# The first microseconds of an encoder layer: first weight pieces on GpSimd's queue, one conversion on VectorE, another source for the warm-up, the identity made later

## The chip, the core and the metric

The kernel runs on one core of one Trainium2 chip. A core has TensorE (PE: matrix products, with PEld for loading the stationary operand), VectorE (DVE), ScalarE (ACT) and GpSimd (POOL), which work in parallel, each through its own instructions in order, and SyncE (SP), which here only issues transfers. Transfers between device memory and on-chip memory run on 16 transfer engines. Those issued by SP go through one queue (q1 in the profile), those issued by GpSimd through another (q0). The metric is the device time of one execution in microseconds; the time given for a kernel is the median over its runs.

## What is computed

One encoder layer on 1024 positions of 1024 channels, in float32: a SwiGLU feed-forward with 2752 hidden channels, a mixer (dilated window attention in three head groups beside a Fourier branch), a second feed-forward, each followed by a scaled residual sum and a layer norm.

```python
h = LN1(alpha*x + 0.5*SwiGLU_a(x))
h = LN2(alpha*h + HybridMixer(h))
h = LN3(alpha*h + 0.5*SwiGLU_b(h))
# SwiGLU(x) = (silu(x @ w_gate) * (x @ w_up)) @ w_down
```

Only the first products of SwiGLU_a, which use x and the first columns of its gate weights, are touched by most of the change.

## The kernel before

**Products.** Every float32 operand is split into a high part (rounded to the matrix engine's float32 form, tile names ending in h) and a low part (the rest, ending in l). A product is then three terms: high by high, high by low, low by high (`TERMS`). High parts are made by a copy, nearly always on ScalarE; low parts by a subtraction on VectorE, which needs the high part. Larger products are computed from seven block products instead of eight; the first block of x is called a11.

**Order.** Nothing in the program is ordered by hand beyond a few constants. The products are jobs in a fixed order for TensorE; the work on VectorE (`V`), ScalarE (`S`) and GpSimd (`G`), and the loads (`Q`), are nodes with dependences, an estimated duration, and a due time taken from the job that needs them. The class `Flow` walks through the jobs with an estimated clock for each engine and for the transfers and emits each node where it fits; each engine's instructions then run on the chip in the order in which they were emitted, and semaphores are derived from the tiles that they read and write. `pool_dma` issues a transfer on GpSimd and tells `Flow` that GpSimd is taken for 0.57 us. Half-size tiles come from a rotating pool of 14 (`half`), large ones from a pool of 46 pages.

**The first step.** The first feed-forward starts with three column blocks of the gate weights (`FIRST = 3`), 128 columns each, and the four 128-channel slices of a11: `first_step(k)` for k = 0 to 3 issues nine matmuls (three terms by three column blocks) into three banks called Aa. Its operands are four pieces of x (`xa`, 256 KB each, high parts Xa110h and Xa111h, two slices in each) and four weight pieces (`fw0` to `fw3`, 192 KB each, from `firsts_w`), made by `first_weights(k)`: a load on SP, a high part on ScalarE, a low part on VectorE. For k = 0 the 384 columns are cut at 128, so that the first column block is converted by an instruction of its own; the other pieces are converted whole. The loads of x and of the weights alternate on SP: x piece, weight piece, x piece, and so on. Behind them SP issues the other blocks of x (`in_xt`) and further weights (`lda`).

**The warm-up.** Before the first step TensorE multiplies a constant by itself eight times (line 2753, each a float32 matmul of 128 by 128 that the profile shows as two). The constant is `one`, a tile of one column that VectorE sets at line 334. The program's own preamble (line 2840) also sets constants on GpSimd, among them a float32 column of 1.0.

**The identity.** At lines 335 to 338 GpSimd counts (iota, tile `jp`, a half-size tile) and VectorE compares, which gives `ident`, a 128 by 128 identity that TensorE uses for transposes and GpSimd once at the very end. Its first reader is the transpose of the biases, `b_ps` (line 1299), whose operands GpSimd loads after the first product of the seventh pair of column blocks (`J[("a", 6), 1]`, numbered from 0) has been planned.

Of the kernel before, what the change touches and what calls it, by code (L numbers as in the profile page):

```python
# [12 lines left out]
AF = mybir.ActivationFunctionType  # L13
OP = mybir.AluOpType
AX = mybir.AxisListType

P = 128
# [27 lines left out]
FIRST = 3  # L45
# [36 lines left out]
class Flow:  # L82
# [22 lines left out]
    def V(self, *a, **kw):  # L105
        return self.task("V", *a, **kw)

    def S(self, *a, **kw):
        return self.task("S", *a, **kw)

    def G(self, *a, **kw):
        return self.task("G", 0.0, *a, **kw)
# [8 lines left out]
    def Q(self, need, mb, fn, deps=(), lead=24.0, **kw):  # L121
        self.loads.append(Node("Q", mb, fn, deps, need, lead, **kw))
        return self.loads[-1]

    def F(self, us, fn, deps=(), banks=0, **kw):
        self.floats.append(Node("F", us, fn, deps, banks=banks, **kw))
        return self.floats[-1]
# [162 lines left out]
class Builder:  # L290
# [7 lines left out]
    def page(self, name, dt=F32):  # L298
        return self.sb.tile([P, 1024], dt, name=name, tag="pg", bufs=NPG)

    def half(self, name, dt=F32):
        return self.sb.tile([P, 512], dt, name=name, tag="s2", bufs=NS2)
# [4 lines left out]
    def bank(self, name):  # L307
        return self.pp.tile([P, 512], F32, name=name, tag="ps", bufs=8)
# [6 lines left out]
def kernel(  # L315
# [6 lines left out]
    nc = tc.nc  # L322
    kb = Builder(ctx, tc)
    fl = Flow()
    page, half, bank = kb.page, kb.half, kb.bank
    V, S, G, Q, F, job = fl.V, fl.S, fl.G, fl.Q, fl.F, fl.job
# [3 lines left out]
    def as_k(t, kd=KD):  # L330
        return t.rearrange("p (k n) -> p k n", k=kd)

    one = kb.small([P, 1], "one")
    nc.vector.memset(one, 1.0)
    ident = kb.small([P, P], "ident")
    jp = half("jp", mybir.dt.int32)[:, :P]
    nc.gpsimd.iota(jp, pattern=[[1, P]], base=0, channel_multiplier=-1)
    nc.vector.tensor_scalar(ident, jp, 0.0, None, op0=OP.is_equal)
    zero = kb.small([P, 1], "zero")
    nc.vector.memset(zero, 0.0)  # L340
    ln_cols = kb.small([P, 32], "ln_cols")
# [3 lines left out]
    def pool_dma(*a, us=0.57, **kw):  # L345
        fl.queued(0.95 if "accum_op" in kw else us, 4e-6 * math.prod(a[0].shape))
        nc.gpsimd.dma_start(*a, **kw)  # L347
# [8 lines left out]
    W, B, H, J = {}, {}, {}, {}  # L356
# [245 lines left out]
    def first_weights(k, need, lead):  # L602

        st = {}

        def load():
            st["r"] = half(f"fw{k}")
            nc.sync.dma_start(st["r"][:, :FIRST * P], firsts_w[k])

        def hi(c0, c1):  # L610
            if c0 == 0:
                st["h"] = half(f"fw{k}h", F32R)
            nc.scalar.activation(st["h"][:, c0:c1], st["r"][:, c0:c1], AF.Copy)

        def lo(c0, c1):
            if c0 == 0:
                st["l"] = half(f"fw{k}l", F32R)
                FWP[k] = st["h"], st["l"]
            nc.vector.tensor_sub(st["l"][:, c0:c1], st["r"][:, c0:c1], st["h"][:, c0:c1].bitcast(F32))
        n, cuts = [(Q(need[0], 0.19, load, lead=lead, halves=1), -2.3)], [0, P, FIRST * P] if k == 0 else [0, FIRST * P]  # L620
        m = []
        for c0, c1 in zip(cuts, cuts[1:]):
            us = 0.15 + (c1 - c0) * 0.95e-3
            n = [S(us, lambda c0=c0, c1=c1: hi(c0, c1), n, need[k], tail=0.9, halves=int(c0 == 0))]
            m = [V(us, lambda c0=c0, c1=c1: lo(c0, c1), n + m, need[k], tail=0.2, halves=int(c0 == 0), hgives=int(c1 == cuts[-1]))]

    def lead_jobs(cs, X, nxt, steps=None):
# [650 lines left out]
    def mixer_consts():  # L1278
        st = {}

        def loads():
            st["raw"] = half("b_raw")[:56, :P]
            pool_dma(st["raw"], b_in.rearrange("(j p) -> j p", p=P))
            st["rb"], st["oh"] = kb.small([NUM_BUCKETS, NH], "rb"), half("oh")[:NUM_BUCKETS, :OH]
            pool_dma(st["rb"], rel_bias)
            pool_dma(st["oh"], c_onehot)
            pool_dma(chan, c_chan)
            pool_dma(ln_cols, c_ln)

        def rounded():  # L1290
            h, l = st["rbs"] = [kb.small([NUM_BUCKETS, NH], f"rb{x}", F32R) for x in "hl"]
            nc.vector.tensor_copy(h, st["rb"])
            nc.vector.tensor_sub(l, st["rb"], h.bitcast(F32))
            st["ohr"] = half("ohr", F32R)[:NUM_BUCKETS, :OH]
            nc.vector.tensor_copy(st["ohr"], st["oh"])

        def products():
            st["ps"], st["ln"] = bank("b_ps"), bank("ln_ps")
            nc.tensor.transpose(st["ps"][:, :56], st["raw"], ident[:56, :56])
            for i, w in enumerate(st["rbs"]):  # L1300
                nc.tensor.matmul(st["ln"][:NH, :OH], w, st["ohr"], start=i == 0, stop=i == 1)

        def columns():
            nc.vector.tensor_copy(b_cols, st["ps"][:, :56])

        def lines(g):
            line = half(f"line{g}")[:NH]
            nc.vector.memset(line, NEG_INF)
            nc.vector.tensor_copy(line[:, MID - HALFW:MID + HALFW + 1], st["ln"][:NH, g * NOFF:(g + 1) * NOFF])
            pool_dma(lines_d[:, g, :], line)  # L1310

        def shears(h):
            src = lines_d[h, h // SLOTS, :]
            pool_dma(shear_d[h], bass.AP(tensor=src.tensor, offset=src.offset, ap=[[0, P], [1, LINE]]))
        q = G(loads, [J[("a", 6), 1]], slack=20.0, halves=2)
        f = F(0.5, products, [V(0.7, rounded, [(q, 20.0)], halves=1)], 2, hgives=3)
        V(0.2, columns, [f], frees=1)
        for g in range(3):
            n = V(0.6, lambda g=g: lines(g), [f], frees=g // 2, halves=1)
            fl.later(n, 5.0, hgives=1)  # L1320
        return [G(lambda h=h: shears(h), [(n, 6.0 + 3.0 * h)]) for h in range(NH)]

    def reversed_rows():
        idx = kb.small([P, 2], "rev_idx", mybir.dt.int32)
        st, n = {}, G(lambda: pool_dma(idx, c_rev), [J[("a", 8), 1]], slack=20.0)
        for t in range(2):
            def gather(t=t):
                st[t] = page(f"rev{t}")
                fl.queued(1.06)
                nc.gpsimd.indirect_dma_start(out=st[t], out_offset=None, in_=w_pf,  # L1330
                                             in_offset=bass.IndirectOffsetOnAxis(ap=idx[:, t:t + 1], axis=0))

            def store(t=t):
                pool_dma(w_rev[t * P:(t + 1) * P, :], st[t])
            n = G(gather, [(n, 20.0)], slack=20.0, pages=1)
            n = G(store, [(n, 30.0)], slack=20.0)
            fl.later(n, 6.0, gives=1)
        return n

    shear_n = mixer_consts()  # L1340
    rev_n = reversed_rows()

# [51 lines left out]
    for i, (to, x0, x1) in enumerate((("t1", "b11", "b12"), ("t3", "b12", "b22"), ("t2", "t1", "b22"),  # L1394
# [6 lines left out]
        n = Q(J[("a", 1 + i), 4], 1.15, copy, [vtn[x0]] if x0 in vtn else [], lead=0.0)  # L1401
# [9 lines left out]
    for i, (to, x0, x1) in enumerate((("t1", "b11", "b12"), ("t3", "b12", "b22"), ("t2", "t1", "b22"),  # L1411
# [11 lines left out]
        n = Q(J[("a", 5 + i), 4], 0.6, copy, [ttn[x0]] if x0 in ttn else [], lead=0.0)  # L1423
# [31 lines left out]
    for p, bk, new in VORDER:  # L1455
        n = PROD[p][1]
# [255 lines left out]
    for i in range(2):  # L1712
        us = {}
# [383 lines left out]
    for i, (to, x0, x1) in enumerate((("t1", "b11", "b12"), ("t3", "b12", "b22"), ("t2", "t1", "b22"),  # L2097
# [6 lines left out]
        n = Q(SUMS0AT[i][0], 1.15, copy, [wtn[x0]] if x0 in wtn else [], lead=0.0)  # L2104
# [69 lines left out]
    for r, n in enumerate(("b11", "b21", "b22", "t1", "t3", "t2", "t4")):  # L2174
        for i in range(2):
            k = 4 * r + 2 * i
# [92 lines left out]
    for gi in range(4):  # L2269
        st = {}  # L2270
# [6 lines left out]
        for i in range(2):  # L2277
# [9 lines left out]
            def hi(gi=gi, i=i, st=st, views=views, t_=t_):  # L2287
                if (t_, i) not in fold:
                    t = page(f"fold{t_}{i}", F32R)
                    fold[t_, i] = t[:, 0:512], t[:, 512:1024]  # L2290
                pv = st["ps", i].rearrange("p (q m) -> p q m", q=4)
                nc.scalar.activation(next(views(i)), pv[:, :, 0:64], AF.Copy)
# [10 lines left out]
            n = S(0.42, hi, [f], pages=1 if s_ == 0 else 0, slack=2.0)  # L2303
# [43 lines left out]
    for t in range(2):  # L2347
        st = {}
# [68 lines left out]
    n = V(0.3, mid_edges, [f], frees=1, slack=2.0)  # L2417
    n = S(1.35, mid_hi, [n], slack=2.0)
# [18 lines left out]
    n = V(0.6, mid_raw, [PJ[2]], pages=1, slack=20.0)  # L2437
    n = S(1.06, mid_hi_w, [(n, 5.0)], pages=1)
# [83 lines left out]
    for c in range(8):  # L2522
        c2, cc = divmod(c, 2)
        st = {}
# [52 lines left out]
        n = S(0.62, sine, [FJ[c]], frees=int(c < 6 and c not in SINE.values()), halves=1)  # L2577
        (seeds if c > 5 else sines)[c - 6 if c > 5 else c] = [None, n]
        n = V(1.8, outs, [n], frees=2, hgives=1, pages=1)
# [4 lines left out]
    for c in range(8):  # L2584
        n, merge = four_out[c]
        n = V(1.38, merge, [n] + pj_n[c], gives=2, pages=2 if c % 2 == 0 else 0)
# [71 lines left out]
    for m in range(8):  # L2658
        n, y = norm_tile(lambda m=m: ya[m], lambda m=m: lw[m], done[m], f"y2_{m}", 2, 16.0 if m > 3 else -8.0)
# [89 lines left out]

    fl.seal()  # L2750
    junk = bank("warm")
    for i in range(8):
        nc.tensor.matmul(junk[:, :P], one.to_broadcast([P, P]), one.to_broadcast([P, P]), start=True, stop=True)
    fl.run()


# [97 lines left out]
```

## Time and profile before

| | us |
|---|---|
| median of 3 runs | 2012.93 |
| lowest, highest | 2012.84, 2013.2 |
| the profiled execution | 2013.17 |
| its span, first to last instruction | 2011.4 |
| busy in it: TensorE | 2005.1 |
| VectorE | 1402.3 |
| ScalarE | 883.7 |
| GpSimd | 366.0 |

The profiled execution's time is 1.77 us longer than its span; the profile's times count from the span's start. A row of the timeline gives the start, the duration, the engine, the line, the operation, the tiles (written from read), how many instructions are merged in it, and in brackets the idle time before it and what ended it. A row of waits names who waited, for whom, the total in us, how often, and the longest. A row of transfer issues gives the tiles, the queue, the count, the size of each, and the median time from issue to landing. In a row of the windows the stretch is followed by its sum, the busy time and the instructions of each engine, the granted TensorE clock, the busy share of the transfer engines and the GB/s that they moved.

### The profile page before, as it was taken

Reading aid. Unit: us, or ns where it says so; the run is one execution under the profiler, and the core shown is the slowest. Engines: PE = TensorE matmul, PEld = TensorE weight load, DVE = VectorE, ACT = ScalarE, POOL = GpSimd, SP = SyncE. Lnnn points to the kernel's source line nnn. Section 1 sums busy time; section 2 is a strip of 40 time slices with the busy share of each in tenths; the row PEclk is TensorE's granted clock in tenths of the full one; section 3 lists DMA queues with packets and bytes.
Section 4 is the critical chain, followed back from the end, with each engine's and each line's share of the span. In section 5 each row is a group of like instructions: output and inputs, shape, how many; then the busy total and the mean of one; then the engine's idle time right before and its main releaser. Section 6 shows DMA issues by size and latency. Waiting matters only on the chain.

```text
span 2011.4 us, 26489 instructions
## 1 busy us (share of the span) xinstructions
PE 2005.1 (100%) x9397; PEld 1680.9 (84%) x9397; DVE 1402.3 (70%) x2066; ACT 883.7 (44%) x1371; POOL 366.0 (18%) x616
## 2 busy tenths in 40 slices
PE   9999999999999999999999999999999999999998
PEld 8888888888888898888888888888888888888887
DVE  8765765577677878776776776877877665575566
ACT  6333333455445224565455445237533333354432
POOL 0133311111011032544443110000011111110000
PEclk9999999999999999999999999999999999999999
DMA  5789988799885286787667779873258877668753
GB/s 209 239 269 281 310 294 260 226 361 401 308 234 192 87 294 218 228 262 201 181 176 233 245 248 354 306 291 147 96 190 255 249 236 229 179 219 285 233 186 97
DMA packets 221829, 478.22 MB, mean 238 GB/s; under 512 B 44606, under 2 KB 95886, under 8 KB 221152
## 3 DMA queue, kind: packets, MB, share of 16 engines
q1 hardware_dynamic: 168736, 310.70, 45.0%
q0 software_dynamic: 52960, 165.82, 27.9%
q8 instruction: 74, 1.21, 0.2%
q14 instruction: 59, 0.48, 0.1%
HBM read 352.98 MB, written 193.68 MB: 272 GB/s over the span
## 4 chain that ended last, share of the span: by engine, by line
PE 100%; DVE 0%; DVEq 0%; issue 0%
PE Ab L541 14%; PE Aa L541 14%; PE Aq L541 8%; PE Db L541 6%; PE Da L541 6%; PE As L541 5%; PE Dq L541 3%; PE Zb L973 3%; PE Xb L973 3%; PE Za L973 3%; PE Xa L973 3%; PE Ds L541 2%; PE wA L2604 2%; PE pv L1939 2%; PE Vb L973 1%; PE Yb L973 1%
## 5 line engine op out<-in xcount | busy, mean ns | idle before, releaser
L347 POOL DMA_DIRECT2D pd<-px x128 | 78.9, 623 | 51.8 <-DVE px L1879 50.4
L347 POOL DMA_DIRECT2D n_spill<-y x16 | 9.4, 586 | 288.1 <-DVE y L1173 241.7
L347 POOL DMA_DIRECT2D hsba<-t2b x21 | 11.6, 551 | 266.5 <-DVE t2b L832 252.8
L347 POOL DMA_DIRECT2D hsaa<-t2a x21 | 12.9, 613 | 235.7 <-DVE t2a L832 230.0
L1870 ACT ACTIVATE p<-p,stat 128x192 f32<-128x192 f32 (+1 forms) x96 | 39.2, 410 | 28.1 <-DVE stat L1865 26.1
L828 DVE TENSOR_TENSOR t2b<-Db,t2b 128x512 f32<-128x512 f32 x21 | 14.5, 691 | 39.0 <-PE Db L541 39.0
L735 ACT ACTIVATE t2b<-Ab 128x512 f32<-128x512 f32 x21 | 12.6, 600 | 63.8 <-PE Ab L541 63.8
L735 ACT ACTIVATE t2a<-Aa 128x512 f32<-128x512 f32 x21 | 12.6, 600 | 61.6 <-PE Aa L541 61.6
L828 DVE TENSOR_TENSOR t2a<-Da,t2a 128x512 f32<-128x512 f32 x21 | 14.5, 689 | 34.0 <-PE Da L541 34.0
L2694 POOL TENSOR_SCALAR zd<-ident,ls 128x128 f32<-128x128 f32 x1 | 0.4, 375 | 202.1 <-DVE ls L2703 202.1
L1158 ACT ACTIVATE y<-ya,ls 128x1024 f32<-128x1024 f32 x16 | 18.4, 1149 | 36.6 <-DVE ls L1153 26.0
L820 DVE TENSOR_TENSOR t3b<-Db,t3b 128x512 f32<-128x512 f32 x21 | 14.5, 691 | 22.2 <-PE Db L541 20.7
L820 DVE TENSOR_TENSOR t3a<-Da,t3a 128x512 f32<-128x512 f32 x21 | 14.5, 691 | 21.7 <-PE Da L541 20.6
L541 PE MATMUL Da<-Xs40h,usa 128*128 128x512 f32 x84 | 29.3, 389 | 0.0
L541 PE MATMUL Da<-Xs41h,usa 128*128 128x512 f32 x84 | 29.3, 389 | 0.0
L541 PE MATMUL Db<-Zs40h,usb 128*128 128x512 f32 x84 | 29.3, 389 | 0.0
L541 PE MATMUL Db<-Zs41h,usb 128*128 128x512 f32 x84 | 29.3, 389 | 0.0
L347 POOL DMA_DIRECT2D gate_d<-os x16 | 8.6, 538 | 94.2 <-ACT os L1629 69.7
L347 POOL DMA_DIRECT2D y_spill<-n x16 | 8.8, 549 | 91.5 <-DVE n L1189 91.4
L735 ACT ACTIVATE t3b<-Ab 128x512 f32<-128x512 f32 x21 | 12.6, 600 | 26.0 <-PE Ab L541 25.8
L735 ACT ACTIVATE t3a<-Aa 128x512 f32<-128x512 f32 x21 | 12.6, 598 | 22.7 <-PE Aa L541 22.6
L1634 DVE SCALAR_TENSOR_TENSOR oq<-Dq,b_cols,t2q 128x512 f32<-128x512 f32 x12 | 11.8, 986 | 13.3 <-PE Dq L541 13.3
(7711 smaller groups left out, 7543.0 us busy)
## 6 DMA issues: line engine op xcount, KB each, us to landing
qa<-hsas SPq DMA_DIRECT2D x43, 256.0 KB, 5.7
qa<-tdat SPq DMA_DIRECT2D x43, 256.0 KB, 5.2
qb<-hsbs SPq DMA_DIRECT2D x43, 256.0 KB, 3.9
ga<-in_ffn_gu_dram SPq DMA_DIRECT2D x21, 512.0 KB, 8.8
ua<-in_ffn_gu_dram SPq DMA_DIRECT2D x21, 512.0 KB, 9.3
gb<-in_ffn_gu_dram SPq DMA_DIRECT2D x21, 512.0 KB, 4.8
ub<-in_ffn_gu_dram SPq DMA_DIRECT2D x21, 512.0 KB, 6.8
qb<-tdbt SPq DMA_DIRECT2D x33, 256.0 KB, 4.3
```

What stands on the lines that cost most here:

```text
L347: nc.gpsimd.dma_start(*a, **kw)
L541: nc.tensor.matmul(out, pick(w, a)[:, k * P:(k + 1) * P], self.cols(xn, b, k), start=first and k == 0 and ti == 0, stop=last and k == kt - ...
L735: nc.scalar.activation(H[c, t], B[c, "B"], AF.Copy)
L820: nc.vector.tensor_sub(H[c, "t3"], B[c, "D"], H[c, "t3"])
L828: nc.vector.tensor_sub(H[c, "t2"], B.pop((c, "D")), H[c, "t2"])
L973: nc.tensor.matmul(bank_, a, b, start=first and ti == 0, stop=last and ti == len(todo) - 1, skip_group_check=True)
L1158: nc.scalar.activation(st["y"], st["a"], AF.Square, bias=s[:, 2:3], scale=1.0, accum_out=s[:, 3:4])
L1634: stt(views(pages_[i], hf), views(b, None), bias[i], views(H.pop((c, t)), None), op0=OP.add, op1=op)
L1870: nc.scalar.activation(p3()[:, i, :], p3()[:, i, :], AF.Exp, bias=stats[h][:, k, 0:1], scale=1.0, accum_out=stats[h][:, k, 1:2])
L1939: nc.tensor.matmul(out, v, pt[:, sl * P:(sl + 1) * P], start=start, stop=stop, skip_group_check=True)
L2604: nc.tensor.matmul(B["w", bk, m], X4.cols(xn, a, k)[:, m * P:(m + 1) * P], pick(w, b), start=new and k == 0 and ti == 0, stop=k == 3 and t ...
L2694: nc.gpsimd.tensor_scalar(st["d"], ident, s()[:, 0:1], -1.0 / D, op0=OP.mult, op1=OP.mult)
```

## The change

Four things are changed.

- The four first weight pieces are issued by GpSimd (`pool_dma`) instead of SP. The four first x pieces and all later loads stay on SP.
- Where a high part of a first weight piece ends at column 128, which is the first cut of piece 0 alone, it is made by VectorE with a copy instead of by ScalarE; the planner gets it as a node of VectorE.
- The warm-up multiplies the preamble's float32 constant, broadcast to 128 by 128, instead of the tile `one`; the memset of `one` goes.
- The identity isn't made at the start. `identity()` registers a node for GpSimd (the iota, after the first product of pair ("a", 6), with its half-size tile taken from the planner's pool) and one for VectorE (the compare) behind it.

```diff
-    one = kb.small([P, 1], "one")
-    nc.vector.memset(one, 1.0)
     ident = kb.small([P, P], "ident")
-    jp = half("jp", mybir.dt.int32)[:, :P]
-    nc.gpsimd.iota(jp, pattern=[[1, P]], base=0, channel_multiplier=-1)
-    nc.vector.tensor_scalar(ident, jp, 0.0, None, op0=OP.is_equal)
...
             st["r"] = half(f"fw{k}")
-            nc.sync.dma_start(st["r"][:, :FIRST * P], firsts_w[k])
+            pool_dma(st["r"][:, :FIRST * P], firsts_w[k])
 
         def hi(c0, c1):
             if c0 == 0:
                 st["h"] = half(f"fw{k}h", F32R)
-            nc.scalar.activation(st["h"][:, c0:c1], st["r"][:, c0:c1], AF.Copy)
+            if c1 == P:
+                nc.vector.tensor_copy(st["h"][:, c0:c1], st["r"][:, c0:c1])
+            else:
+                nc.scalar.activation(st["h"][:, c0:c1], st["r"][:, c0:c1], AF.Copy)
...
-            n = [S(us, lambda c0=c0, c1=c1: hi(c0, c1), n, need[k], tail=0.9, halves=int(c0 == 0))]
+            n = [(V if c1 == P else S)(us, lambda c0=c0, c1=c1: hi(c0, c1), n, need[k], tail=0.9, halves=int(c0 == 0))]
...
+    def identity():
+        jp = {}
+
+        def count():
+            jp["t"] = half("jp", mybir.dt.int32)[:, :P]
+            nc.gpsimd.iota(jp["t"], pattern=[[1, P]], base=0, channel_multiplier=-1)
+        n = G(count, [J[("a", 6), 1]], slack=20.0, halves=1)
+        V(0.3, lambda: nc.vector.tensor_scalar(ident, jp["t"], 0.0, None, op0=OP.is_equal), [(n, 1.0)], slack=20.0, hgives=1)
+
+    identity()
     shear_n = mixer_consts()
...
     junk = bank("warm")
+    ones = nc.const_aps.tensor(1.0, (P, P))
     for i in range(8):
-        nc.tensor.matmul(junk[:, :P], one.to_broadcast([P, P]), one.to_broadcast([P, P]), start=True, stop=True)
+        nc.tensor.matmul(junk[:, :P], ones, ones, start=True, stop=True)
```

## The prediction

> **What bounds the kernel now.** I read the page first, then the table of waits for TensorE, then the timeline of the first 14 us.
>
> ```profile
> span 2011.4 us, 26489 instructions
> PE 2005.1 (100%) x9397; PEld 1680.9 (84%) x9397; DVE 1402.3 (70%) x2066; ACT 883.7 (44%) x1371; POOL 366.0 (18%) x616
> ...
> PE zr L2697 <- POOL zd L2694: 1.4, 1, 1.4
> PE warm L2753 <- DVE one L334: 0.9, 1, 0.9
> ...
> 0.28 0.10 POOL L2840 MEMSET const-float32-1.0<- 128x1 f32 x1
> ...
> 0.73 0.39 SPq L1244 DMA_DIRECT2D xa<-in_firsts_dram  x1
> 0.81 0.06 DVE L334 MEMSET one<- 128x1 f32 x1 [0.81 <-PEq L2840]
> 0.84 0.23 POOL L337 IOTA jp<- 128x128 int32 x1 [0.40 <-POOLq L2840]
> ...
> 0.92 3.79 PE L2753 MATMUL warm<-one 128*128 128x128 f32 x16 [0.92 <-DVE one L334]
> 1.11 0.23 DVE L338 TENSOR_SCALAR ident<-jp 128x128 f32<-128x128 int32 x1 [0.24 <-POOL jp L337]
> 1.18 0.42 SPq L608 DMA_DIRECT2D fw<-in_firsts_w_dram  x1
> ...
> 3.46 0.63 ACT L395 ACTIVATE Xa110h<-xa 128x512 fp32r<-128x512 f32 x1 [1.45 <-DMA xa<-in_firsts_dram]
> ...
> 4.00 0.60 ACT L613 ACTIVATE fw0h<-fw 128x128 fp32r<-128x128 f32 x2
> 4.01 0.43 SPq L608 DMA_DIRECT2D fw<-in_firsts_w_dram  x1
> 4.12 0.69 DVE L401 TENSOR_TENSOR Xa110l<-xa,Xa110h 128x512 fp32r<-128x512 f32 x1 [2.77 <-ACT Xa110h L395]
> ...
> 4.36 1.63 PE L599 MATMUL Aa<-Xa110h,fw0h 128*128 128x512 f32 x3
> 4.49 0.43 SPq L1244 DMA_DIRECT2D xa<-in_xt_dram  x1
> ...
> 5.79 1.46 PE L599 MATMUL Aa<-Xa110l,fw0h 128*128 128x512 f32 x3
> 6.10 0.63 ACT L395 ACTIVATE Xa110h<-xa 128x512 fp32r<-128x512 f32 x1 [1.50 <-DMA xa<-in_firsts_dram]
> 6.64 0.51 ACT L613 ACTIVATE fw1h<-fw 128x384 fp32r<-128x384 f32 x1
> ...
> 7.07 0.88 PE L599 MATMUL Aa<-Xa110h,fw0l 128*128 128x512 f32 x3
> 7.79 0.86 PE L599 MATMUL Aa<-Xa110h,fw1h 128*128 128x512 f32 x3
> ...
> 14.08 0.40 PE L541 MATMUL Aa<-Xa120h,lda0h 128*128 128x512 f32 x1
> ```
>
> TensorE works in 2005.1 of 2011.4 us, and its whole list of waits is two rows: 0.9 us before the warm-up and 1.4 us behind the last tile. All that the change can gain therefore lies in the first microseconds, and all that it could lose later would have to be a wait that the kernel does not have now.
>
> In those first microseconds three things follow one another. The first piece of x is awaited until 3.46 and its high part made by 4.09 (3.46 + 0.63). ScalarE then makes fw0h in two parts, until 4.60. TensorE starts its first useful product at 4.36, when the first part is there. From 7.79 to 14.08 lie 27 products (steps 1 to 3, nine each): 0.233 us each. From 5.79 to 7.07 lie three: 0.427 us each. So TensorE runs its first six products at not much over half its later pace, and the full pace begins at about 7.07, 6.15 us after the warm-up began. Step 0 (nine products) takes 7.79 - 4.36 = 3.43 us where the full pace would need 9 x 0.233 = 2.10. From 4.36 to 5.79 there are 1.43 us for three products, 1.28 at the slow pace: 0.15 us went to waiting for the second part of fw0h.
>
> One microsecond of earlier start in the slow stretch is 1/0.427 = 2.34 products more before the pace changes, each of which saves 0.233 us behind it: **an earlier start is worth 0.545 of itself**, and so is a late one.
>
> **The change part by part.** The profiled execution took 2013.17 us, its span and 1.77 us around it; the median of the three runs is 2012.93, 0.24 less. The sum is made as a difference against the profiled execution, and then put on the median.
>
> *Warm-up with the preamble's constant.* The constant 1.0 is written by 0.38, so the wait for VectorE's memset (0.81 to 0.87) is gone. What is left is the start of the program, which releases SP at 0.73. The warm-up starts about 0.17 earlier, at 0.75, and with its 3.79 us ends at about 4.54. The useful products don't wait for it then. If the full pace also comes 0.17 earlier, that is worth 0.17 x (1 - 0.233/0.427) = 0.08; if not, nothing. I take 0.04.
>
> *Four weight pieces on GpSimd's queue.* Removed from SP are four issues of 0.42 to 0.43 us. SP's later issues move up by one to four slots of about 0.47: the second x piece by one, the first large x transfer from 4.49 to about 2.6. GpSimd no longer has the iota at its start, so its first issue comes at about 0.80 and the four take these durations:
>
> ```profile
> 60.83 0.75 POOL L347 DMA_DIRECT2D hsaa<-t2a  x1 [59.75 <-DVE t2a L832]
> 71.48 0.56 POOL L347 DMA_DIRECT2D hsaa<-t2a  x1 [9.90 <-DVE t2a L832]
> ...
> xa<-in_firsts_dram SPq DMA_DIRECT2D x1, 256.0 KB, 2.7
> fw<-in_firsts_w_dram SPq DMA_DIRECT2D x1, 192.0 KB, 2.7
> ...
> out_dram<-z SPq DMA_DIRECT2D x1, 256.0 KB, 2.1
> ...
> hsbs<-sab POOLq DMA_DIRECT2D x2, 256.0 KB, 2.3
> ...
> DMA to landing us min/median/max: 2.5/4.6/7.6
> ...
> chan<-in_c_chan_dram POOLq DMA_DIRECT2D x1, 256.0 KB, 7.1
> ...
> 3.00:4.00 1.00, 1.00 (x6) 1.00 (x6) 0.00 (x0) 0.54 (x2) 0.00 (x0) 1.00 1.04 261
> 4.00:5.00 1.00, 1.00 (x6) 0.97 (x5) 0.88 (x3) 0.60 (x3) 0.00 (x0) 1.00 0.89 152
> 5.00:6.00 1.00, 1.00 (x4) 0.81 (x3) 0.35 (x2) 0.00 (x0) 0.00 (x0) 1.00 0.89 313
> ```
>
> The first GpSimd issue of the program takes 0.75, a later one 0.56: they end at 0.80 + 0.75 + 3 x 0.56 = 3.23. The fourth piece is issued at about 2.7 instead of 4.01. No load by GpSimd into an idle machine is in the trace. The nearest rows: a 256 KB store by GpSimd in a quiet stretch lands in 2.3 us, one by SP in 2.1; GpSimd's loads of a bias tile (the line of minimum, median and maximum) land in 2.5 at the least and 4.6 in the median; the load of chan, queued behind others, took 7.1. SP's own two first loads take 2.7. I take 2.7 to 3.1 for the first weight piece, near the quiet rows, because nothing but the first x piece is then in flight: it lands at 3.5 to 3.9, against 1.18 + 2.7 = 3.88 now. The ends are 3.3 (0.80 + 2.5) and 7.9 (0.80 + 7.1).
>
> What it costs: the first x piece (256 KB, landed at 3.43) has the transfer engines to itself today, and the weight piece follows. Now both are in flight together. At worst they share evenly and both land when the second of them lands now, at 3.88; the same bytes need the same time. Then Xa110h is made from 3.91 to 4.54 and TensorE starts at 4.57. At best the x piece is undisturbed and TensorE starts at 4.12. I take the middle, 4.35. The pieces for step 1 have room: fw1h is ready at 6.64 + 0.51 = 7.15 and is needed at 7.79. The three windows (their last two numbers) show the transfer engines busy at 0.89 to 1.04 while only 152 to 313 GB/s flow, so earlier issues on SP mostly wait in a queue that is full already.
>
> The Trainium skill ("DMA: Bandwidth & Descriptors", Specifications) speaks against this part: it puts the first byte of a GpSimd transfer at about 1 us and of an SP one at about 0.6. By that estimate the piece lands 0.4 later than on SP, at 3.9, and the start is 4.57; the rows show 0.2 between the two queues.
>
> *First high part on VectorE.* Removed from ScalarE: the first of the two fw0h instructions. Added to VectorE: a conversion of 128 columns.
>
> ```profile
> L1295 DVE CAST ohr<-oh 32x388 fp32r<-32x388 f32 x1 | 0.3, 344 | 0.0
> L1292 DVE CAST rbh<-rb 32x12 fp32r<-32x12 f32 x1 | 0.2, 154 | 0.0
> ```
>
> Between 0.154 for 12 columns and 0.344 for 388, that is 0.21. VectorE is idle until 4.12, so it runs beside Xa110h. ScalarE's second part, 0.40, then follows Xa110h directly and is ready 0.40 after it, before the second product asks for it (0.427): the 0.15 us of waiting are gone. Behind the new instruction on VectorE stands Xa110l, which the fourth product needs 1.28 us after the start; the copy and Xa110l together take 0.90 from the landing, so this never binds. Should Xa110l stand ahead of it in the order, fw0h would come at 5.0; the planner counts the weight piece as there before it counts Xa110h as made, so I don't expect that.
>
> *Identity in the sixth pair.* An iota of 0.23 on GpSimd and a compare of 0.23 on VectorE leave the start and come back near 111 us.
>
> ```profile
> DVE t12a6l L372 <- ACT t12a6h L367: 1.1, 1, 1.1
> ...
> L1299 PE MATMUL b_ps<-ident,b_raw x1: 265/265/265, 142.1 to 142.1; 56*128 56x56 f32 x1
> ```
>
> VectorE idles 1.1 us before one instruction there, GpSimd had idled 9.90 us before its issue at 71.48 and idles as long between its groups, and the identity is first read at 142.1, some 30 us later. Cost nothing; without that cover 0.23 us on VectorE. At the start it frees GpSimd before its first issue, counted above.
>
> *Sum*: start at 4.35 and no gap, (4.36 + 0.15 - 4.35) x 0.545 = 0.09 gained, with 0.04 from the warm-up 0.13. At the ends: start 4.12 with the earlier pace gains 0.21 + 0.08 = 0.29, start 4.57 without it loses 0.03. From 2013.17 that gives 2013.04; on the median, **2012.8**, with 2012.6 to 2013.0 as its own bounds and 0.3 more on each side for runs that spread from 2012.84 to 2013.2.
>
> **The rivals.**
>
> *R1, the weight piece lands late, nothing else.* For: 4.6 us is GpSimd's median in the bias row. It would land at 5.4 and TensorE start at about 5.67, (5.67 - 4.51) x 0.545 = 0.63 lost; a landing at 4.9 loses 0.36. Against: those loads ran beside others. Time 2013.2 to 2013.6.
>
> *R2, slower: a hole in TensorE's work holds the slow pace longer.* Place: between the end of the warm-up, now 4.54, and the first product. Today there is none, since 4.36 lies before the warm-up's end at 4.71. It decides from the point where the weight piece lands after about 4.3 (4.54 less the copy's 0.21), which the forecast's late end just touches. If the hole restarts the 6.15 us, a start at 5.2 brings the full pace at 11.35 instead of 7.07: 4.28 x 0.454 = 1.94, with 0.38 for the late start 2.3. Time **2015.2**. Against: the landing must be late and the count must restart, and no row shows either.
>
> *R3, the full pace a whole step earlier.* The warm-up starts 0.17 earlier; if the pace changes in steps of a clock that the kernel doesn't set, this may reach an earlier one, before step 0. Then its nine products take 2.10 instead of 3.43: 1.33 less, and 2011.5. For: the runs differ by 0.36 among themselves. Against: 0.17 is small beside 6.15.
> The Trainium skill ("TensorE: Matmul & The Clock Gate", The HAM clock gate) gives a free-running window of about 3.4 us that must be busy before full speed. With a start at 0.92 full speed would come between 4.3 and 7.7; the 7.07 here agrees. By it R2 costs one window, 3.4 x 0.454 = 1.5, so 2014.8, and R3 stays possible.
>
> *R4, the rest of the order changes.* The planner decides by estimated times, and a changed start may shift later decisions. For: VectorE, ScalarE and GpSimd get other estimates. Against: TensorE waits for nothing in the middle of the kernel, so there is slack for small shifts. A weight load issued so late that its landing lies bare costs up to 8.8 us:
>
> ```profile
> ga<-in_ffn_gu_dram SPq DMA_DIRECT2D x21, 512.0 KB, 8.8
> ```
>
> That would be 2021.7; the likelier size is below 2.
>
> **How the numbers follow.** Forecast 0.65, R1 0.11, R2 0.11, R3 0.08, R4 0.05. The predicted time is the forecast's, 2012.8. The range 2011.4 to 2013.9 holds the forecast, R1 and R3; R2 and R4, 0.16 together, are left out. A measurement of this kernel can tell 0.2%, 4.0 us, from no change. No case gains that much: the start holds 1.33 us of slow pace and 0.9 of waiting in all. Faster 0.02, for what I have not seen; slower 0.04, the heavy end of R4; the rest is within.
>
> **What would show it.** In the timeline after: the four fw issues on GpSimd between 0.8 and 3.2; the warm-up from about 0.75; fw0h on VectorE before Xa110l; the first useful product at 4.1 to 4.6 and step 1 at 7.5 to 7.8. The identity near 111 us with VectorE waiting as before. A first product after 5 shows R1, products of 0.427 us after 8 us show R2, products of 0.233 in step 0 show R3, and a new row among TensorE's waits shows R4. A time beyond 2013.9 with none of these, or a gain beyond 1.5 us, would prove the reading wrong.

## The result and the profile after

| | kernel before | changed kernel |
|---|---|---|
| median, us | 2012.93 (2012.22 to 2013.65, 14 runs) | 2016.99 (2014.89 to 2019.2, 14 runs) |
| ratio | 1 | 1.0021, 95% interval 1.0014 to 1.0028 |
| profiled execution: time, span | 2013.17, 2011.4 | 2017.23, 2015.5 |

The change costs 4.06 us, in the medians and in the two profiled executions alike. The changed kernel also spreads more: 4.3 us between its fastest and slowest run, against 1.4.

First the table of TensorE's waits in the changed kernel (engine, line, what it waited for: us in total, times, longest).

```profile
PE Aa L594 <- DVE fw0h L609: 2.5, 1, 2.5
PE zr L2705 <- POOL zd L2702: 1.4, 1, 1.4
PE warm L2762 <- PEq L2849: 0.8, 1, 0.8
PE sc L1842 <- DVE oq L1642: 0.2, 1, 0.2
```

A new wait leads it, 2.5 us in front of the first step, for the high part of the first weight piece. The timeline of the changed kernel shows how it came about (start, duration, engine, line, tiles, idle before and releaser; line 342 issues GpSimd's transfers, 609 is the conversion on VectorE, 594 the first steps).

```profile
0.73 1.81 SPq L1242 DMA_DIRECT2D xa<-in_firsts_dram  x4
...
0.77 3.74 PE L2762 MATMUL warm<-const-float32-1.0 128*128 128x128 f32 x16 [0.77 <-PEq L2849]
...
1.29 2.35 POOL L342 DMA_DIRECT2D fw<-in_firsts_w_dram  x4 [0.85 <-POOLq L2849]
...
3.38 0.63 ACT L390 ACTIVATE Xa110h<-xa 128x512 fp32r<-128x512 f32 x1 [1.37 <-DMA xa<-in_firsts_dram]
...
6.64 0.23 DVE L609 CAST fw0h<-fw 128x128 fp32r<-128x128 f32 x1 [5.74 <-DMA fw<-in_firsts_w_dram]
...
7.01 0.95 PE L594 MATMUL Aa<-Xa110h,fw0h 128*128 128x512 f32 x3 [2.50 <-DVE fw0h L609]
...
7.78 1.47 PE L594 MATMUL Aa<-Xa110l,fw0h 128*128 128x512 f32 x3
...
9.04 1.48 PE L594 MATMUL Aa<-Xa110h,fw0l 128*128 128x512 f32 x3
...
10.32 1.26 PE L594 MATMUL Aa<-Xa110h,fw1h 128*128 128x512 f32 x3
...
11.42 0.84 PE L594 MATMUL Aa<-Xa110l,fw1h 128*128 128x512 f32 x3
...
16.86 0.39 PE L536 MATMUL Aa<-Xa120h,lda0h 128*128 128x512 f32 x1
```

From the view of the tile fw, the time from issue to landing of the four weight pieces:

```profile
DMA to landing us min/median/max: 5.3/6.5/7.3
```

GpSimd's first issue comes at 1.29, not 0.80, and the first piece is there at 6.64, 5.3 after its issue. The x piece is not delayed: its high part starts at 3.38, against 3.46 before. The warm-up ends at 4.51, so TensorE has nothing to do for 2.50 us. Then a second thing happens: the first three products run at the full pace, and from 7.78 to 11.2 TensorE is back at half. The view by stretches of 1 us says the same in the granted clock (stretch, then busy shares with counts of PE, PEld, DVE, ACT and POOL, the granted TensorE clock, the transfer engines' share, GB/s).

```profile
4.00:5.00 1.00, 0.51 (x3) 0.23 (x2) 0.00 (x0) 0.01 (x1) 0.00 (x0) 1.00 0.65 189
5.00:6.00 1.00, 0.00 (x0) 0.00 (x0) 0.00 (x0) 0.00 (x0) 0.00 (x0) 1.00 0.97 309
6.00:7.00 1.00, 0.00 (x0) 0.02 (x1) 0.36 (x2) 0.36 (x2) 0.00 (x0) 1.00 0.97 374
7.00:8.00 1.00, 0.99 (x4) 0.89 (x5) 1.00 (x4) 0.57 (x2) 0.00 (x0) 0.89 1.03 371
8.00:9.00 1.00, 1.00 (x3) 0.76 (x3) 0.78 (x3) 0.73 (x2) 0.00 (x0) 0.50 0.98 381
...
11.00:12.00 1.00, 1.00 (x5) 0.79 (x5) 0.64 (x3) 1.00 (x2) 0.00 (x0) 0.90 1.05 397
```

(The column reads 1.00 also where the clock record has not begun yet; the pace of the products shows the half clock of the first microseconds.) The trace's clock records put the full clock at 4.37 to 7.78, half at 7.78 to 11.20 and full from there on: 3.413 us each. In the kernel before, the full clock begins at 7.08 and stays until after the last product.

At the first product on lda0h the changed kernel is 2.78 us late (16.86 against 14.08 in the prediction's rows). This stays constant to within 0.1 us until about 900 us; TensorE then loses 0.8 more, and the rest is lost at the end. The last rows, of the changed kernel and then of the kernel before, are:

```profile
2009.92 1.13 PE L2705 MATMUL zr<-ln3g,zd 128*128 128x512 f32 x2 [1.42 <-POOL zd L2702]
```
```profile
2006.33 1.12 PE L2697 MATMUL zr<-ln3g,zd 128*128 128x512 f32 x2 [1.42 <-POOL zd L2694]
```

That is 3.59 late. The span is 4.1 longer, so 0.5 is lost behind the last product. So the three losses are **2.8 at the start, 0.8 near 900 us, 0.5 behind the end**; the experiments ask what belongs to which part of the change.

### The profile page after: what moved, and what is told of

The parts are those of the page before. It is cut to its first block, busy times and chain, and to the rows that moved or that the text cites. A ratio compares the mean times of both kernels' runs of the same rounds, so it can differ in the third digit from the quotient of the medians.

```text
span 2015.5 us, 26493 instructions
## 1 busy us (share of the span) xinstructions
PE 2006.1 (100%) x9397; PEld 1681.0 (83%) x9397; DVE 1402.2 (70%) x2066; ACT 884.5 (44%) x1370; POOL 367.6 (18%) x620
## 4 chain that ended last, share of the span: by engine, by line
PE 98%; DVE 1%; DMA 1%; SPq 0%; issue 0%; ACT 0%; DVEq 0%; POOLq 0%
PE Ab L536 14%; PE Aa L536 14%; PE Aq L536 7%; PE Db L536 6%; PE Da L536 6%; PE As L536 5%; PE Za L971 3%; PE Zb L971 3%; PE Xb L971 3%; PE Xa L971 3%; PE Dq L536 3%; PE Ds L536 2%; PE wA L2612 2%; PE pv L1947 2%; PE Vb L971 1%; PE Yb L971 1%
```

## The experiments

The theory was that GpSimd's queue brings the first piece late, which starts the work late and opens a hole that lets the clock fall. Against it stood: that the other three parts of the change carry some of it; that the early x pieces now crowd the transfer engines, whatever the queue; that the piece is merely too large; and, from the second group of runs on, a rival about the loss near 900 us. The times, each beside the kernel before on the same chip:

| run | what differs from the changed kernel | median us (range) | ratio, 95% interval |
|---|---|---|---|
| e0_after | nothing | 2017.13 (2015.59 to 2018.28) | 1.0021, 1.0012 to 1.0030 |
| e1_sp | weight pieces on SP | 2013.21 (2012.73 to 2014.31) | 1.0003, 0.9994 to 1.0012 |
| e5_act | weight pieces on ScalarE's queue | 2012.64 (2012.29 to 2015.53) | 1.0001, 0.9992 to 1.0010 |
| e2_pool_only | the other three parts undone | 2016.9 (2014.31 to 2018.17) | 1.0018, 1.0009 to 1.0027 |
| e4_first_on_sp | first piece alone on SP | 2014.34 (2014.01 to 2015.5) | 1.0008, 0.9999 to 1.0017 |
| e6_split_first | first piece in two transfers | 2018.13 (2017.06 to 2019.15) | 1.0024, 1.0014 to 1.0034 |
| e3_warm20 | 20 warm-up products | 2018.08 (2017.21 to 2019.69) | 1.0026, 1.0016 to 1.0037 |
| e11_pool_wide8 | 8 warm-up products, 320 columns | 2015.57 (2014.87 to 2017.94) | 1.0015, 1.0006 to 1.0024 |
| e8_sp_warm20 | on SP, 20 warm-up products | 2017.89 (2016.52 to 2019.61) | 1.0025, 1.0015 to 1.0034 |
| e9_sp_wide8 | on SP, 8 of 320 columns | 2014.98 (2014.22 to 2015.52) | 1.0011, 1.0002 to 1.0020 |
| e10_sp_narrow20 | on SP, 20 of 48 columns | 2021.76 (2019.52 to 2022.71) | 1.0045, 1.0032 to 1.0059 |

The kernel before had medians of 2012.83, 2012.99 and 2012.86 in the three groups.

### The changed kernel again

No edit.

> The changed kernel itself, a second look. If the late first weight piece is a property of the kernel, it lands again after 6.0 us and the first useful product starts at 6.5 to 7.5, the median is 2016 to 2018 and the runs spread over 3 us or more. If the landing at 6.6 us was chance, it lands before 4.5 in this profile. If the 0.87 us that the first profile lost near 900 us and the 0.45 us at the end belong to the change, they are there again in the same places; if they are chance, at least one is gone.

Measured: +4.30 us, and a wait of 3.2 in front of the first step. The start costs 3.5 here (late by that much from 16 us on), the stretch near 900 us 0.03, and the end 0.44. So the loss at the end is there again, the one at the start moves by some tenths between runs, and the one near 900 us comes and goes.

### Only the queue undone

```diff
-            pool_dma(st["r"][:, :FIRST * P], firsts_w[k])
+            nc.sync.dma_start(st["r"][:, :FIRST * P], firsts_w[k])
```

> The changed kernel with the four weight pieces issued by SP again; the VectorE conversion, the warm-up's constant and the late identity stay. If the queue move costs the time (by whatever way), the first product starts at 4.1 to 4.4 and the median is 2012.5 to 2013.0, not above before. If one of the other three parts costs it, the median stays above 2015. Rival: a part of it each, 2014.

Measured: +0.38 us, no difference that can be told, though the median lies 0.2 above the expected stretch. Rows of its timeline:

```profile
4.01 0.23 DVE L609 CAST fw0h<-fw 128x128 fp32r<-128x128 f32 x1 [3.11 <-DMA fw<-in_firsts_w_dram]
...
4.38 1.46 PE L594 MATMUL Aa<-Xa110h,fw0h 128*128 128x512 f32 x3
```

So conversion, warm-up and identity together cost and bring nothing that shows, and the 4 us are the queue's. The conversion takes 0.23 us on VectorE (0.21 in the prediction); the identity is made at 111.3 and 118.6 us and read at 141.5.

### Only the queue changed

The kernel before, with this alone:

```diff
-            nc.sync.dma_start(st["r"][:, :FIRST * P], firsts_w[k])
+            pool_dma(st["r"][:, :FIRST * P], firsts_w[k])
```

> The kernel before with one part of the change alone: the four weight pieces issued by GpSimd; the vector for the warm-up, the conversion on ScalarE and the identity stay as they were, so that GpSimd's iota stands ahead of its first issue. Theory (GpSimd's queue itself is late in the first microseconds): the first piece lands near 6.6 us, first useful product near 7.1, TensorE's work shifted by 2.5 to 3.7 us, median 2016 to 2017.5. Rival (the late issue at 1.29 is a price of the rest of the change, not of GpSimd's queue): the first issue at 0.80 to 1.0, the piece at 4 to 5.5, median 2013 to 2014.5.

Measured: +3.91 us. Here GpSimd makes the identity's iota before its first issue. Rows of the timeline, and from the view of the tile fw the time from issue to landing:

```profile
0.84 0.23 POOL L337 IOTA jp<- 128x128 int32 x1 [0.40 <-POOLq L2840]
...
1.40 2.37 POOL L347 DMA_DIRECT2D fw<-in_firsts_w_dram  x4 [0.33 <-issue]
...
7.46 1.04 PE L599 MATMUL Aa<-Xa110h,fw0h 128*128 128x512 f32 x3 [2.76 <-ACT fw0h L613]
```
```profile
DMA to landing us min/median/max: 5.7/6.1/7.0
```

The theory holds: the queue alone brings the late piece, a wait of 2.76 us and the time. The rival on the late issue falls: with the iota ahead the first issue is at 1.40, without it at 1.29, and in neither order at the 0.80 of the prediction. GpSimd is through with the iota at 1.07 and still issues nothing until 1.40.

### Another queue than SP's, not GpSimd's

```diff
-            pool_dma(st["r"][:, :FIRST * P], firsts_w[k])
+            nc.scalar.dma_start(st["r"][:, :FIRST * P], firsts_w[k])
```

> The changed kernel with the four weight pieces issued by ScalarE's queue, another queue beside SP's like GpSimd's, with SP's four x pieces just as early. If GpSimd's queue itself is late (issue at 1.29, first packet 2 us later), the first weight piece lands here at 3.4 to 4.3 and the median is 2012.5 to 2013.5. If the early x pieces crowd out any second queue, it lands at 5.5 or later here too and the median is above 2015. ScalarE's own issues may delay its first conversion by up to 1 us, which would be 0.5 us of the time.

Measured: -0.19 us, no difference. Rows of the timeline, and the time to landing from the view of the tile fw:

```profile
0.73 1.85 ACTq L603 DMA_DIRECT2D fw<-in_firsts_w_dram  x4
...
4.30 0.23 DVE L609 CAST fw0h<-fw 128x128 fp32r<-128x128 f32 x1 [3.41 <-DMA fw<-in_firsts_w_dram]
...
4.81 1.04 PE L594 MATMUL Aa<-Xa110h,fw0h 128*128 128x512 f32 x3 [0.59 <-ACT Xa110h L390]
```
```profile
DMA to landing us min/median/max: 3.5/5.2/7.0
```

The pieces now compete with the x pieces of SP's queue, from 0.73 on, and the first lands 3.5 us after its issue, ready to be converted at 4.30. The x piece is late as well: its high part starts at 4.13, against 3.38 in the changed kernel. So sharing with the x pieces is the likely price of the 0.8 above the 2.7 of the kernel before; ScalarE's queue without them was not run. The other 1.8 of GpSimd's 5.3, and the issue at 1.29 in place of 0.73, come with that queue. Of the 1.8, 0.6 lies ahead of its first packet, which starts at 3.36, 2.1 us after the issue; on ScalarE's queue it is 1.4 (0.73 to 2.17). How much of the rest is a slower queue, and how much the transfers that SP has in flight by then, no run separates.

### The first piece alone on SP

```diff
-            pool_dma(st["r"][:, :FIRST * P], firsts_w[k])
+            (nc.sync.dma_start if k == 0 else pool_dma)(st["r"][:, :FIRST * P], firsts_w[k])
```

> The changed kernel with the first of the four weight pieces back on SyncE's queue and the other three on GpSimd's. Theory (only the first piece's landing sets the start; the other pieces have 1.4 us of work each in front of them): the first product near 4.4 us, then a wait for the second piece of 0.5 to 2 us if that lands near 7.5, too short or too late to hold the clock down for a whole window; median 2013 to 2015. Rival (any use of GpSimd's queue at the start costs the 4 us, through its later transfers and the end): 2016 to 2017.5, with the stall near 893 us and the end 0.4 us longer.

Measured: +1.35 us; the interval touches no change. Rows of the timeline, and one of TensorE's table of waits:

```profile
3.92 0.40 ACT L611 ACTIVATE fw0h<-fw 128x256 fp32r<-128x256 f32 x1
...
4.28 1.62 PE L594 MATMUL Aa<-Xa110h,fw0h 128*128 128x512 f32 x3
...
5.69 1.34 PE L594 MATMUL Aa<-Xa110l,fw0h 128*128 128x512 f32 x3
```
```profile
PE Aa L594 <- ACT fw1h L611: 0.5, 1, 0.5
```

The start is the early one again, the second piece is awaited for 0.5 us (expected 0.5 to 2), and the clock does not fall. Most of the loss hangs on the first piece. One part of the rival holds: the end is 0.37 longer than before the change here too, though only three pieces go through GpSimd's queue. These rows also correct the prediction's 0.15 us of waiting for the second part of fw0h: that part is ready at 4.32 here, far before the second product needs it, and the first three products still take 1.41 us (5.69 - 4.28), as before the change (1.43). There was no such wait, and the prediction's own rows say so: the second part was there at 4.60 and needed at 4.36 + 0.427 = 4.79.

### The first piece in two transfers

```diff
-            pool_dma(st["r"][:, :FIRST * P], firsts_w[k])
+            for a, b in [(0, P), (P, FIRST * P)] if k == 0 else [(0, FIRST * P)]: pool_dma(st["r"][:, a:b], firsts_w[k][:, a:b], us=0.57 * (b - a) / FIRST / P)
```

> The changed kernel with the first weight piece issued by GpSimd as two transfers, the 64 KB of the first product ahead of the other 128 KB. Rival (the piece is late because 192 KB take long on that queue): the 64 KB land a third of the way, near 4.6 us, first product near 5, median near 2014. Theory (the queue is late as a whole: no packet before about 3.25 us, the first ones slow): the 64 KB land at 5.5 or later, first product at 6 to 6.9, median 2015.5 to 2017.2.

Measured: +5.14 us, a median 1.1 above the changed kernel's, with ranges that overlap. The view of the transfers (count, size, median us to landing) and TensorE's waits:

```profile
fw<-in_firsts_w_dram POOLq DMA_DIRECT2D x1, 128.0 KB, 5.3
fw<-in_firsts_w_dram POOLq DMA_DIRECT2D x1, 64.0 KB, 3.8
```
```profile
PE Aa L594 <- ACT fw0h L611: 1.6, 1, 1.6
...
PE Aa L594 <- DVE fw0h L609: 0.9, 1, 0.9
```

Both sides missed. 64 KB still take 3.8 us on that queue, 2.2 of them ahead of its first packet (1.28 to 3.46), against 2.7 for three times as much on SP: most of it does not depend on the size. But they come 1.5 earlier than 192 KB, so size is not nothing. The single product that could start earlier splits the hole in two, 0.9 and 1.6, and in this execution the clock record gives full speed only from 13.42 us on. The start costs 4.5 us in it, against 2.8 and 3.5 with one hole, and the stretch near 900 us 1.0. Whether two short holes are always worse than one, a single profile doesn't show.

### Filling the hole

Twenty warm-up products in place of eight (e3), or eight that are wider (e11):

```diff
-    for i in range(8):
+    for i in range(20):
```
```diff
-    ones = nc.const_aps.tensor(1.0, (P, P))
+    ones, cols = nc.const_aps.tensor(1.0, (P, P)), nc.const_aps.tensor(1.0, (P, 320))
     for i in range(8):
-        nc.tensor.matmul(junk[:, :P], ones, ones, start=True, stop=True)
+        nc.tensor.matmul(junk[:, :320], ones, cols, start=True, stop=True)
```

> The changed kernel with 20 warm-up products instead of 8, so that TensorE has work until about 6 to 7 us, while the weights still land late. If the hole in TensorE's work makes the clock fall again, as the profile after suggests, no product of step 0 takes 0.427 us after 8 us and 1.0 to 1.8 us of the loss go: median 2014.8 to 2015.8, with a spread below 2 us. If the late landing alone costs the time and the slow products are only the usual start, the median stays at 2016.5 to 2017.5 with the same spread.

> The changed kernel (weight pieces on GpSimd's queue) with the hole filled by eight wide warm-up products (320 columns each) and no instruction added to TensorE's stream. The first product at 7 to 8.7 us, no wait above 0.5 us ahead of it, no fall of the clock behind it. Theory B: no stall near 893 us above 1 us, so the time is that of the late start alone, 2014.5 to 2016.2, under the changed kernel's 2017. Theory A: the stall as with twenty products, 2017 to 2018.5.

Measured: 2018.08 with twenty, 2015.57 with eight wide ones. In both the first product comes late (7.31 and 6.77) and the clock, once full, does not fall. Rows of e11's timeline:

```profile
0.77 6.40 PE L2762 MATMUL warm<-const-float32-1.0 128*128 128x320 f32 x16 [0.77 <-PEq L2849]
...
6.77 1.10 PE L594 MATMUL Aa<-Xa110h,fw0h 128*128 128x512 f32 x3
...
7.70 0.86 PE L594 MATMUL Aa<-Xa110l,fw0h 128*128 128x512 f32 x3
...
15.20 0.39 PE L536 MATMUL Aa<-Xa120h,lda0h 128*128 128x512 f32 x1
```

It reaches lda0h at 15.20, 1.12 late. Its first product came 0.24 earlier than in the changed kernel (7.01), so of the 2.78 there about 1.36 is the late start at full pace and **1.4 is the fallen clock**. The medians agree: filling the hole brings 1.4 to 1.6 us (2015.57 against 2016.99 and 2017.13). With twenty products the gain at the start is there as well (late by 1.5 instead of 2.8), but TensorE loses 3.9 us near 900 us, which nobody had expected.

### The loss near 900 us

e3 left three readings: that the four transfers on GpSimd's queue disturb later ones, that the late work as such does, or that the twelve added instructions do. e8 puts the pieces on SP with twenty warm-up products; e9 does so with eight wide ones; e10 with twenty narrow ones of 48 columns (diffs as above, with the SP line of e1).

> The changed kernel with all four weight pieces on SyncE's queue and twenty warm-up products in place of eight, so that useful work starts about as late as with GpSimd's queue, at 6.9 to 7.1 us, but without that queue and without a hole. Theory (the stall of 4 us near 893 us and the longer end, seen with twenty warm-up products, belong to the four transfers on GpSimd's queue): no stall, TensorE shifted by 0.8 to 1.6 us throughout, median 2013.8 to 2014.8. Rival (the stall belongs to the shift of all work by about 1.4 us): the stall is there again, median 2017 to 2018.5.

> The weight pieces on SyncE's queue and the warm-up as long as with twenty products, but made of eight wide ones (320 columns each), so that TensorE has as many instructions as the changed kernel. Both theories have useful work start at 6.9 to 8.7 us, TensorE shifted by 0.8 to 3.0 us. Theory A (a shift of all work of 1 to 2 us is what makes the transfers of 840 to 893 us late): the stall near 893 us is there again, median 2017 to 2018.5. Theory B (twelve more instructions on TensorE move the places at which its instructions are fetched, and a fetch near 843 us delays a chain of transfers): no stall, median 2014 to 2015.5.

> The weight pieces on SyncE's queue and twenty warm-up products of 48 columns, together about as long as the eight of 128, so that twelve instructions are added to TensorE's stream and next to no time. Both theories have the first product near 4.4 us. Theory A (shift of the work): no stall near 893 us, median 2012.5 to 2013.8 as with eight products. Theory B (place of the instruction fetches): the stall is there, TensorE shifted by 2.5 to 4 us from 900 us on, median 2015.5 to 2017.

e8 and e9 agree at the start: no GpSimd load, no hole, and lda0h is reached at the same time. Of e8 the waits (TensorE's, and one of ScalarE's between 880 and 900 us) and two rows of the timeline:

```profile
PE Aq L536 <- ACT Aq L728: 1.7, 1, 1.7
...
PE Dq L536 <- DVE oq L1642: 0.8, 1, 0.8
...
ACT gq7h L362 <- DMA gq<-in_in_pairs_dram: 3.8, 1, 3.8
```
```profile
14.98 0.39 PE L536 MATMUL Aa<-Xa120h,lda0h 128*128 128x512 f32 x1
...
2010.88 1.12 PE L2705 MATMUL zr<-ln3g,zd 128*128 128x512 f32 x2 [1.42 <-POOL zd L2702]
```

The same of e9, where TensorE's list has two rows only:

```profile
PE zr L2705 <- POOL zd L2702: 1.4, 1, 1.4
PE warm L2762 <- PEq L2849: 0.8, 1, 0.8
```
```profile
14.99 0.39 PE L536 MATMUL Aa<-Xa120h,lda0h 128*128 128x512 f32 x1
...
2007.22 1.13 PE L2705 MATMUL zr<-ln3g,zd 128*128 128x512 f32 x2 [1.42 <-POOL zd L2702]
```

e8's median lies where its rival, the shift of all work, had put it. With twenty products the load of gq comes 3.8 us after ScalarE is ready for it, with eight it is there in time; 3.66 us part the two ends (2010.88 and 2007.22), 2.9 the medians, and the ranges don't touch. e3 and e11 are a second such pair, with GpSimd's queue: 3.9 us near 900 and none, 2.5 between the medians. So neither GpSimd's queue nor the late work makes this stall: the theory in e8's expectation and theory A fall. What differs within each pair is the make-up of the warm-up alone: twelve products more (the profile shows each as two), and narrower ones. SP issues gq behind transfers that wait for stores and reloads between on-chip and device memory, and in e8 and e3 a step of that chain lasts longer (SP's longest wait for it between 836 and 856 us is 6.4 and 6.5 us, against 5.2 in e9 and 5.4 in e11). In the view of the transfers from 841 to 845 us e8 has a row that e9 has not:

```profile
q8 instruction: 1, 0.02, 2.9%
```

It is a transfer of 16 KB of instructions, which the trace has at 842.0 in e8 and at 846.0 in e9, while that chain runs. That the added products move this transfer, as theory B has it, is seen; that it is what delays the chain was not shown, and e10 speaks against its being enough.

e10 missed its purpose. The narrow products don't take less time: forty of them last 8.74 us, from 0.77 on. Each still loads its 128 by 128 operand, and these loads keep PEld busy for 8.61 us, 0.215 each, where the sixteen of the kernel before took 3.49, 0.218 each. And although TensorE was not idle from 0.77 on, the clock record has full speed only from 12.85 us on.

```profile
0.77 8.74 PE L2762 MATMUL warm<-const-float32-1.0 128*128 128x48 f32 x40 [0.77 <-PEq L2849]
...
9.30 1.63 PE L594 MATMUL Aa<-Xa110h,fw0h 128*128 128x512 f32 x3
```

The first product came at 9.30, at half pace, which alone makes TensorE 5.1 us late; the stall near 900 us took 1.0 us in its profile. Both theories had the start wrong. Something on B can still be read from it. With each run's own lateness taken off, the 16 KB transfer comes at 841.1 to 842.6 us in e8, e3 and e10, which have twenty products, and at 845.2 to 845.7 in e9, e11, the changed kernel and the kernel before. So it moves with the number of products in e10 too, and still the loss is 1.0 there, against 3.6 in e8 and 3.9 in e3, and the changed kernel loses 0.8 without any move. The profiled run of e10 is the fastest of its five, by 1.6 us or more, so the others may have lost more there. The cause of this stall stays open.

## Why the prediction was wrong

The forecast was 2012.8, and the time 2016.99, outside the range. What came is rival R2, at 2015.2 with a chance of 0.11, and about 1.8 us more. The prediction's own signs of R1 and R2 are both there: the first product after 5, at 7.01, and products of about 0.42 us after 8 us.

**What bounds the kernel**: right. The losses are waits and a slow stretch that the kernel did not have; TensorE's instructions are the same.

**The four pieces on GpSimd's queue: the step that failed**, in both terms. The issue was put at 0.80, about where the iota had stood, and came at 1.29. The landing was taken as 2.7 to 3.1 us after the issue, "near the quiet rows", with 2.5 and 7.1 as ends, and was 5.3 (4.8 in e11, 5.7 in e2, 6.0 in e0). The rows chosen were stores and SP's loads; of GpSimd's own loads the bias row had a median of 4.6, which was kept for R1 at 0.11, and chan took 7.1. Other loads by GpSimd in the kernel before, near 112 us, landed in 6.2 to 6.9 (b_raw, rb, oh, ln_cols). By the queue's own median the piece lands at 5.4 even from 0.80, as R1 had it, and that is past the 4.3 from which R2 decides: R1 and R2 were one case, with 0.22 between them, and should have been the forecast. Crowding between weight and x pieces, which the prediction did weigh, is 0.8 us at most on ScalarE's queue and costs no time that can be told there.

**R2's mechanism**: shown, its size a little off. A hole of 2.5 us does let the clock fall; with the hole filled it doesn't. The prediction let the 6.15 us start anew, to 11.35; half speed ended at 11.20, but that the two lie close is luck. It was not a restart: the clock was full at first (4.37 to 7.78) and then half for one window of 3.413 us. The useful products began 2.65 us late (7.01 against 4.36) and at full pace, which cost 1.36 where R2, with a start at 5.2, had 0.38; the fall cost 1.4 where R2 had 1.94. The Trainium skill ("TensorE: Matmul & The Clock Gate", The HAM clock gate) has a free-running window of about 3.4 us; the records agree, at 3.413. The time that the prediction made of it, one window of half speed, 1.5 us, is nearly the 1.4 that e11 gives. By the same section of the Trainium skill the clock falls after a window of idle; in this trace 2.5 idle of 3.4 us were enough, and in e2 2.1 (5.35 to 7.46, in a window that ends at 8.76). In e2 a window with 0.65 us of idle (1.94 to 5.35, the warm-up ending at 4.70) still gave full speed; counted back from 7.08 in the same steps, one of the kernel before with 0.67 (0.25 to 3.67, the warm-up starting at 0.92) did not. How much idle a window may hold is not settled here.

The Trainium skill's first byte for GpSimd's queue ("DMA: Bandwidth & Descriptors", Specifications), about 1 us beside 0.6, was the warning that the prediction weighed and set at 0.4 us. Its direction was right; in this trace the first packets of that queue start at 3.36, 2.1 us after the issue, and SP's at 1.75, 1.0 after theirs.

**The 0.545 of an earlier or later start**: true only while the place of the full clock is fixed. Where the window falls differs between the profiled executions (full from 7.08 in the kernel before, 5.49 in e1, 6.72 in e4, 3.77 in e5). In e1 that brings lda0h 0.77 us earlier (13.31 against 14.08), which is of the size of the spread of the kernel before, 1.4; no run shows that it is the spread's cause. Rival R3, an earlier step of the clock, is this: e1's and e5's profiled runs had it, but their medians show no gain.

**Warm-up**: it starts at 0.77 and ends at 4.51, as predicted (0.75 and 4.54), and is worth nothing that shows. **VectorE's conversion**: 0.23 us, 0.21 predicted; the 0.15 us that it was to save were not there. **Identity**: nothing, as predicted.

**R4**: partly. The order of the instructions is unchanged but for those that the change moves, yet a load late by some tenths does lie bare near 900 us in some runs (0.8 in the changed kernel's profile, 0.03 in its repetition). The medians of the changed kernel and of e11 don't tell how often.

**What no case had**: the end. From the start of the last product (the second of the two merged in the last row) to the end of the span it takes 4.54 us before, 4.65 to 4.66 in e1 and e9, 4.88 in e2 and 4.98 to 5.00 in the changed kernel and e11. So 0.34 of the loss comes with the queue, in e2 against before and in the changed kernel against e1, and 0.11 with the other parts. The last output packets end 3.3 to 3.4 us after that product in all of these. What differs is SP's closing list of waits on semaphores, of which each takes 0.06 us: in the kernel before and in e1 the wait for the last output is the last but one entry (at 3.65 and 3.75), in e2 and the changed kernel four more entries stand behind it (it is met at 3.74 and 3.85). Which semaphore stands where differs between the programs whose loads use different queues.

## What to carry to other kernels

The first load of a program, the one that all work waits for, belongs on a queue whose landing the trace shows for a load at the start; a quiet row from the middle, of a store or of another queue, says little about it. A late operand can cost more than its lateness where it empties TensorE for most of a clock window: in the changed kernel a first product 2.65 us late cost 2.78, and with the gap filled one 2.41 late cost 1.12. Fill such a gap, if it can't be closed, with few wide products; many narrower ones went with a further loss in e3 and e8. Among the nearest rows, the one of the same queue and the same direction weighs most.

## What the runs showed of the hardware that was not expected

- GpSimd does not issue its first transfer before 1.28 us in any of these runs, while SP and ScalarE issue at 0.73; its first packets follow 2.0 to 2.2 us later.
- TensorE being occupied is not what grants the clock: under forty products of 48 columns, back to back from 0.77 to 9.5, it stayed at half until 12.85; under warm-ups of 128 or 320 columns that last 6.2 to 6.4 us, in e3, e8, e9 and e11, full speed came between 3.88 and 4.49.
- Twenty warm-up products of 128 columns in place of eight of 320 went with 3.6 and 3.9 us more loss near 900 us in two pairs of runs, with the order of all other work unchanged; twenty of 48 columns went with 1.0 in the one profile of them.
